# A hybrid decoder layer: weight transposes ahead of the scores, key and query splits on VectorE, attention operands loaded earlier

## The chip, the cores and the metric

The kernel runs on 1 core of one Trainium2 chip. The metric is the device time of one execution in microseconds. The kernel before took 1698.91 us (median of 3 runs, 1698.31 to 1705.39).

Engine names as in the profile: PE is TensorE's matmul, PEld its weight load, DVE VectorE, ACT ScalarE, POOL GpSimd, SP SyncE; SPq is SP's queue, from which most transfers are issued.

## The reference

One layer on 1024 tokens of width 1024, all in float32. The input projection feeds two mixers: a Mamba-2 scan of 16 heads (two groups, eight chunks of 128 tokens) and a causal differential attention of 8 heads. Both outputs, side by side 2048 wide, go through the output projection; a gated feed-forward block and norms follow.

```python
n = rmsnorm(h, mix_norm_w); proj = n @ w_in
y_ssd = ssd_mixer(proj[:, :SSD_PROJ], ...)          # chunked scan, gated norm
# attention, per head and block of 128 query rows: two score maps of depth 64
s = einsum("mbhqd,mbhkd->mbhqk", q, k)              # m = 0, 1; q scaled by 64**-0.5
p = softmax(where(causal, s, -inf)); w = p[0] - lam * p[1]
y_da = rmsnorm(w @ v, subln_w) * (1 - lambda_init)  # v is 128 wide
h = h + concat([y_ssd, y_da]) @ w_out
h = h + (silu(n2 @ w_gate) * (n2 @ w_up)) @ w_down  # n2 = rmsnorm(h)
return rmsnorm(h, final_norm_w)
```

## The kernel before

**Precision.** A float32 product is made of three matmuls of split operands. `split(hi, lo, raw)` casts `raw` to a shorter type on ACT (`hi`, the CAST of L173) and subtracts on another engine (`lo = raw - hi`, the TENSOR_TENSOR of L174). `mm3` (L119 to L121) then issues hi·hi, lo·hi and hi·lo. So every operand of a projection goes through a raw buffer, one ACT and one DVE instruction.

**Stages on the profile's axis.** To about 403 us: input norm, then the z, B, C, x and v projections, with the first group's scan woven in. 403 to 583 us: the k and q projections (8 calls of `pair_T`, 7 pieces each, 12 matmuls of 128x512 to a piece), with the second group's scan, `ssd_scan(1)`, woven in by `weave`: after the n-th piece, 30/50·n steps of the scan have been issued (L693 to L695). The scan writes its transposed output `y` to DRAM (`yT_d`), and k and q go to DRAM too. 583 to 969 us: attention. 969 to 1046 us: the rest of the output projection. From there the feed-forward block.

**Attention.** The loop at L940 runs over steps s; step s is head h = s // 8 and block i = s % 8 of 128 query rows; 64 such steps and 5 behind them drain. The step issues the two score maps of (h, i) (`att_front`: L769 with the queries' `QH`, L770 with their `QL`, L772 the causal mask), the row maximum on DVE (`nmx`, L774 or L776) and two exponentials on ACT (L778). Work of earlier rows follows, popped from a table `later` by a key: `att_mix` of row s-1 (DVE, L785 to L788: reciprocal `r`, factor `rr`, mixed weights into `p`), `att_turn` of row s-2 (PE transposes `wtp`, L798, copied back by ACT, L799), then filler matmuls, then `att_back` of row s-2 (PE, L804, output bank `o`), and `att_square`, `att_norm`, `att_out` of row s-3 or a group of four rows (`ms_o`, `of`, `oa` on DVE, transposes `otp`).

**Filler.** Between the turn and the back matmuls stand steps of the output projection (`filler`, `share`), each three matmuls of 128x256 into `po_s`. Phase 1 has 256 such steps, over the first two groups of `y` (y0 to y3, y4 to y7: `yh`, `yl`) with weights `wo0_*` and `wo1_*`; phase 2 has 128, over y8 to y11 (attention heads 0 to 3) with `wo2_*`. `share` gives phase 1 eight steps in each of s = 2 to 17 and 19 to 34, one call at s = 36 that only loads phase 2's operands, and four steps from s = 38 on.

**Orders.** PE's order in attention is that of the code (`manual_schedule` names PE only). The order of DVE, ACT, POOL and SP is fixed when the kernel is built, by a scheduler that plays the instructions through; the code's order is only its input.

**Buffers.** Tiles rotate in pools: P4 has 6 buffers of 4 KB per partition (probabilities `p` in attention), CV 4 (`kd`, `qd`, `v`), A4 14 (`KS`, `QH`, `QL`), B16 4 (`yh`, `yl`). A weight's raw tile, `wr_*`, has two buffers of its own (`load_raw`, L169), shared with the raws of y4 to y11.

**Keys and queries of a head** are loaded in two halves of 512 tokens (`qk_load`) and split (`qk_split`): KS is cast on ACT (L738), its other half-partitions become the low part by two 64x512 subtractions (L179), QH and QL come from `split`. For head 0 the subtractions run on DVE, for the others on GpSimd. Head h's half 0 is loaded at step 8(h-1) and split two steps later, half 1 is loaded at 3 and split at 5.

Of the kernel before, what the change touches and what calls it, by code (L numbers as in the profile page):

```python
# [9 lines left out]
F32 = mybir.dt.float32  # L10
# [7 lines left out]
P = 128  # L18
# [6 lines left out]
def tile_hybrid_block(  # L25
# [24 lines left out]
    nc = tc.nc  # L50
    DM = 1024
    T = 1024
    NT = T // P
# [100 lines left out]
    def CV(shape, dt, name):  # L154
        return cv.tile(shape, dt, tag="cv", name=name)
# [11 lines left out]
    def load_raw(src, shape, name):  # L167
        raw = wp.tile(shape, F32, tag="raw", bufs=2, name="wr_" + name)
        nc.sync.dma_start(raw, src)  # L169
        return raw  # L170
# [122 lines left out]
    nc.vector.memset(ones, 1.0)  # L293


    def w_unit(src, shape, name, alloc=None):
        raw = load_raw(src, shape, name)
        if alloc is None:
            hi = wp.tile(shape, F32R, tag="wh", bufs=3, name="wh_" + name)
            lo = wp.tile(shape, F32R, tag="wl", bufs=3, name="wl_" + name)  # L300
        else:
            hi, lo = alloc(shape, F32R, "wh_" + name), alloc(shape, F32R, "wl_" + name)
        split(hi, lo, raw)
        return hi, lo
# [376 lines left out]
    for col, name, sk in ((C_B, "B", sink_bc("B")), (C_C, "C", sink_bc("C")), (C_X, "x0", sink_x(0)),  # L681
# [3 lines left out]
        if name == "C":  # L685
# [6 lines left out]
    parity[0] = 1  # L692
    weave([(lambda c=c, d=d, n=n, h=h, sc=sc: pair_T(c + h * P, f"{n}{h}", sink_T(d, h), sc), 7)  # L693
           for h in range(0, NH, 2) for c, d, n, sc in ((C_K, kT_d, "k", None), (C_Q, qT_d, "q", 0.125))],
          ssd_scan(1), 30 / 50)  # L695


    cneg = hx.tile([P, P], F32, tag="hx", name="cneg")
# [20 lines left out]

    def qk_load(h, half):  # L720
        sl = slice(half * 512, half * 512 + 512)
        kd, qd = [CV([P, 2, 512], F32, f"{n}d{h}_{half}") for n in "kq"]
        for t_, src in ((kd, kT_d), (qd, qT_d)):
            sv = src[h].rearrange("(m d) t -> d m t", d=64)
            for r in (0, 64):
                nc.sync.dma_start(t_[r:r + 64, :, :], sv[:, :, sl])
        return kd, qd

    def qk_split(h, half, kd, qd):

        eng = nc.gpsimd if h else nc.vector
        ks = A4([P, 2, 512], F32R, f"KS{h}_{half}")
        qh = A4([P, 2, 512], F32R, f"QH{h}_{half}")
        if h or half:
            ql = A4([P, 2, 512], F32R, f"QL{h}_{half}")
        else:
            ql = wp.tile([P, 2, 512], F32R, tag="wl", bufs=3, name=f"QL{h}_{half}")
        nc.scalar.copy(ks, kd)  # L738
        for m in range(2):
            b = slice(64 - 64 * m, 128 - 64 * m)  # L740
            sub(ks[b, m, :], kd[b, m, :], ks[b, m, :].bitcast(F32), eng=eng)
        split(qh, ql, qd, eng)
        return ks, qh, ql
# [47 lines left out]
    def att_turn(h, i, pm):  # L791
        n = f"{h}_{i}"
        wT = pm[1]
        for j0 in range(0, i + 1, 4):
            j1 = min(i + 1, j0 + 4)
            pt = MS([P, 512], f"wtp{n}_{j0}")
            for j in range(j0, j1):
                nc.tensor.transpose(pt[:, (j - j0) * P:(j - j0 + 1) * P], pm[0][:, j * P:(j + 1) * P], ident)  # L798
            nc.scalar.copy(wT[:, j0 * P:j1 * P], pt[:, :(j1 - j0) * P])  # L799

    def att_back(h, i, pm, vt, o):
        wT = pm[1]
        for j in range(i + 1):
            nc.tensor.matmul(o[:, i % 4, :], wT[:, j * P:(j + 1) * P], vt[j], start=(j == 0), stop=(j == i))  # L804
# [13 lines left out]
    def att_out(h, q, oa):  # L818
        pt = MS([P, 512], f"otp{h}_{q}")
        for j in range(4):  # L820
            nc.tensor.transpose(pt[:, j * P:(j + 1) * P], oa[:, j, :], ident)
        if h >= NH // 2:
            if not y3:
                y3.extend(B16([P, 4, T], f"y{e}3") for e in "hl")
            hi, lo = [y[:, h - NH // 2, q * 512:q * 512 + 512] for y in y3]
            sl = pcol[:, SL:SL + 1]
            nc.scalar.mul(hi, pt, sl)
            nc.vector.scalar_tensor_tensor(lo, pt, sl, hi.bitcast(F32), op0=ALU.mult, op1=ALU.subtract)
            return
        oT = oa.rearrange("p j d -> p (j d)")  # L830
        nc.scalar.mul(oT, pt, pcol[:, SL:SL + 1])
        nc.sync.dma_start(yT_d[8 + h, :, q * 512:q * 512 + 512], oT)


    KG = 4
    NG = 16 // KG

    def load_y(kg):
        yh, yl = B16([P, KG, T], f"yh{kg}"), B16([P, KG, T], f"yl{kg}")
        for j in range(KG):  # L840
            kt = kg * KG + j
            if kg == 0:
                raw = P4([P, T], F32, f"wr_y{kt}")
                nc.sync.dma_start(raw, yT_d[kt])
            else:
                raw = load_raw(yT_d[kt], [P, T], f"y{kt}")
            split(yh[:, j, :], yl[:, j, :], raw)
        return yh, yl

    def wo_unit(kg, cg, alloc=None):  # L850
        src = w_out2[kg * KG * P:(kg + 1) * KG * P, cg * 256:cg * 256 + 256].rearrange("(k p) c -> p k c", p=P)
        return w_unit(src, [P, KG, 256], f"wo{kg}_{cg}", alloc)

    def out_steps(t, kys, ws, name, bank=MM):

# [16 lines left out]
    def filler():  # L872

        for kgs in ((0, 1), (2,)):
            nxt = [wo_unit(kg, 0) for kg in kgs]
            ys = [load_y(kg) for kg in kgs]
            yield
            for cg in range(4):
                cc = slice(cg * 256, cg * 256 + 256)
                ws = nxt  # L880
                for t in range(0, NT, 2):
                    if t == 6 and cg < 3:
                        nxt = [wo_unit(kg, cg + 1) for kg in kgs]
                    hx_t = hx.tile([P, 2, 256], F32, tag="hx", name=f"hx_{cg}_{t}_{kgs[0]}")
                    nc.sync.dma_start(hx_t, (h_d if kgs[0] else xh)[:, t:t + 2, cc])
                    steps = out_steps(t, ys, ws, f"s{kgs[0]}{cg}")
                    for q in range(2 * KG * len(kgs)):
                        ps = next(steps)
                        if q == 2 * KG * len(kgs) - 1:
                            nc.vector.tensor_tensor(hx_t, ps, hx_t, op=ALU.add)  # L890
                            nc.sync.dma_start(h_d[:, t:t + 2, cc], hx_t)
                        yield
# [4 lines left out]
    later = {}  # L897

    def at(step, f):
        later.setdefault(step, []).append(f)  # L900
# [16 lines left out]
    split_of(0, 1)  # L917
    for h in range(1, NH):
        s0 = (h - 1) * NT
        for d, f, a in ((0, raw_of, (h, 0)), (2, split_of, (h, 0)), (3, raw_of, (h, 1)), (4, v_of, (h,)),  # L920
                        (5, split_of, (h, 1))):
            at(s0 + d, lambda f=f, a=a: f(*a))
    ROWS = NH * NT

    def fill_up(n):
        for _ in range(n):
            next(fill, None)

    def share(s):

        if 2 <= s < 18 or 19 <= s < 35:
            fill_up(8)
        elif s == 36:
            fill_up(1)
        elif 38 <= s < ROWS:
            fill_up(4)
        elif s >= ROWS:
            fill_up(8)

    with tc.manual_schedule(engines={mybir.EngineType.PE}):  # L940
        for s in range(ROWS + 5):
            h, i = divmod(s, NT)
            if h < NH:
                pm, sm = att_front(h, i, [heads[h][0], heads[h][1]])
                if i % 4 == 0:
                    o = psum["oo"].tile([P, 4, P], F32, tag="oo", name=f"o{h}_{i // 4}")
                    oa = ob.tile([P, 4, P], F32, tag="ob", name=f"oa{h}_{i // 4}")
                    sso = small.tile([P, 4], F32, tag="sso", bufs=2, name=f"sso{h}_{i // 4}")
                    r4 = small.tile([P, 4, 2], F32, tag="r4", bufs=2, name=f"r4{h}_{i // 4}")
                vt = heads[h]["v"]  # L950
                at(s + 1, lambda h=h, i=i, pm=pm, sm=sm, r4=r4: att_mix(h, i, pm, sm, r4[:, i % 4, :]))
                at(s + 2, lambda h=h, i=i, pm=pm: att_turn(h, i, pm))
                at(s + 2.5, lambda h=h, i=i, pm=pm, vt=vt, o=o: att_back(h, i, pm, vt, o))
                at(s + 3, lambda h=h, i=i, pm=pm, o=o, r4=r4, sso=sso: att_square(h, i, pm, o, r4, sso))
                if i % 4 == 3:
                    at(s + 3, lambda h=h, q=i // 4, o=o, oa=oa, r4=r4, sso=sso: att_norm(h, q, o, oa, r4, sso))
                    at(s + 4.5, lambda h=h, q=i // 4, oa=oa: att_out(h, q, oa))
            for f in later.pop(s, []):
                f()
            share(s)  # L960
            for f in later.pop(s + 0.5, []):
                f()
        ws = [wo_unit(3, 0)]
        for _ in fill:
            pass
# [19 lines left out]
    ys = [y3]  # L985
# [329 lines left out]
```

## Time and profile before

| | |
|---|---|
| runs | 1698.31, 1698.91, 1705.39 us |
| profiled execution | 1696.42 us, span 1694.7 us, mean granted clock 0.975 |
| PE | busy 1588.5 us, 94% of the span |
| DVE, ACT, POOL | 1129.5 (67%), 802.4 (47%), 568.2 us (34%) |
| k/q projections, 403.00 to 583.20 | 180.20 us, PE busy 179.86 |
| attention, 583.20 to 969.00 | 385.8 us |
| rest of the output projection, 969.00 to 1046.00 | 77.00 us, PE busy 76.03 |

A stage's window has its length, then the busy time of each engine with its count of instructions, then the clock granted to TensorE as a share of full speed. What PE can gain in a stage is its idle time (length less busy) and the time that it ran at a lower clock.

### The profile page before, as it was taken

How to read it: one execution, taken by the hardware profiler on the slowest of the kernel's cores; microseconds unless marked ns; L12 is line 12 of the kernel's file. 1: busy time of each engine (PE TensorE's matmuls, PEld its weight loads, DVE VectorE, ACT ScalarE, POOL GpSimd, SP SyncE). 2: the span in 40 equal slices, each digit the busy share in tenths (PEclk: the TensorE clock that was granted, in tenths of full speed). 3: DMA queues.
4: the chain of work that ended last, by engine and by line, in shares of the span. 5: the costliest groups of instructions: out<-in, count | busy, mean ns of one | idle time of the engine just before them, and what ended most of it. 6: DMA issues, size and time to landing. Idle time of an engine off the chain costs nothing. (4 is left out here: it accounts for less than half of the span.)

```text
span 1694.7 us, 24141 instructions
## 1 busy us (share of the span) xinstructions
PE 1588.5 (94%) x9034; PEld 1379.4 (81%) x9034; DVE 1129.5 (67%) x1597; ACT 802.4 (47%) x1659; POOL 568.2 (34%) x412
## 2 busy tenths in 40 slices
PE   5999989999999879899789998999999999999997
PEld 4977889898878769899678898888888888778886
DVE  8666787776665565556766658655555555698987
ACT  4544666544444455555665524433333333334445
POOL 5113233234333042222221024444444445542422
PEclk9999999999999979999899999999999999999999
DMA  4213345645545585434433242322332232963222
GB/s 164 88 49 115 109 129 170 190 137 170 169 145 176 157 224 151 122 103 131 156 106 119 91 139 91 105 94 93 107 106 94 93 106 97 358 247 119 99 100 99
DMA packets 160798, 225.24 MB, mean 133 GB/s; under 512 B 10581, under 2 KB 121242, under 8 KB 159274
## 3 DMA queue, kind: packets, MB, share of 16 engines
q1 hardware_dynamic: 157050, 210.53, 38.3%
q0 software_dynamic: 3632, 13.17, 2.5%
q8 instruction: 71, 1.16, 0.3%
q14 instruction: 45, 0.37, 0.1%
HBM read 156.23 MB, written 67.44 MB: 132 GB/s over the span
## 5 line engine op out<-in xcount | busy, mean ns | idle before, releaser
L120 PE MATMUL x<-n,wa 128*128 128x512 f32 x352 | 137.4, 390 | 0.0
L119 PE MATMUL x<-n,wa 128*128 128x512 f32 x352 | 137.3, 392 | 0.0
L121 PE MATMUL x<-n,wa 128*128 128x512 f32 x352 | 136.2, 390 | 0.0
L119 PE MATMUL po_s<-wh_wo,yh 128*128 128x256 f32 x384 | 116.4, 303 | 7.7 <-ACT yh L173 7.7
L173 ACT CAST wa<-s 128x512 fp32r<-128x512 f32 x88 | 54.8, 622 | 130.2 <-PE x L121 58.5
L121 PE MATMUL po_s<-wh_wo,yl 128*128 128x256 f32 x384 | 110.9, 289 | 4.1 <-DVE yl L174 4.1
L778 ACT ACTIVATE p<-s,nmx 128x256 f32<-128x256 f32 (+7 forms) x128 | 94.7, 743 | 42.4 <-DVE nmx L774 26.4
L120 PE MATMUL po_s<-wl_wo,yh 128*128 128x256 f32 x384 | 110.6, 288 | 1.7 <-DVE wl_wo L174 1.7
L174 DVE TENSOR_TENSOR wa<-s,wa 128x512 fp32r<-128x512 f32 x88 | 76.9, 875 | 47.3 <-ACT wa L173 47.0
L804 PE MATMUL o<-v,p 128*128 128x128 f32 x576 | 79.8, 284 | 25.6 <-ACT p L778 7.9
L173 ACT CAST dg<-gd 128x512 fp32r<-128x512 f32 x77 | 47.8, 622 | 113.2 <-PE dx L121 55.6
L804 PEld LDWEIGHTS o<-v,p 128*128 128x128 f32 x576 | 71.7, 195 | 29.6 <-issue 10.5
L769 PE MATMUL s<-KS,QH 128*128 128x512 f32 (+2 forms) x192 | 79.3, 413 | 5.3 <-ACT QH L173 3.2
L119 PEld LDWEIGHTS po_s<-wh_wo,yh 128*128 128x128 f32 x384 | 75.4, 196 | 8.8 <-ACT yh L173 8.8
L121 PEld LDWEIGHTS po_s<-wh_wo,yl 128*128 128x128 f32 x384 | 75.2, 196 | 5.2 <-DVE yl L174 5.2
L174 DVE TENSOR_TENSOR dg<-gd,dg 128x512 fp32r<-128x512 f32 x77 | 63.4, 827 | 23.5 <-ACT dg L173 23.5
L121 PEld LDWEIGHTS x<-n,wa 128*128 128x128 f32 x352 | 66.4, 189 | 13.9
L119 PEld LDWEIGHTS x<-n,wa 128*128 128x128 f32 x352 | 66.4, 189 | 13.6
L120 PEld LDWEIGHTS x<-n,wa 128*128 128x128 f32 x352 | 66.4, 189 | 13.6
L120 PEld LDWEIGHTS po_s<-wl_wo,yh 128*128 128x128 f32 x384 | 75.6, 197 | 1.9 <-DVE wl_wo L174 1.9
L774 DVE TENSOR_REDUCE nmx<-s 128x1 f32<-128x640 f32 (+3 forms) x64 | 63.8, 1019 | 12.7 <-PE s L772 12.1
L120 PE MATMUL dx<-dw,dg 128*128 128x512 f32 x176 | 67.9, 392 | 2.8 <-DVE dw L174 2.7
(491 smaller groups left out, 5213.7 us busy)
## 6 DMA issues: line engine op xcount, KB each, us to landing
gd<-g_d SPq DMA_DIRECT2D x11, 1792.0 KB, 10.1
wr_g<-in_w_gate_dram SPq DMA_DIRECT2D x22, 512.0 KB, 3.6
wr_u<-in_w_up_dram SPq DMA_DIRECT2D x22, 512.0 KB, 3.7
g_d<-sg SPq DMA_DIRECT2D x22, 512.0 KB, 2.6
wr_d<-in_w_down_dram SPq DMA_DIRECT2D x22, 512.0 KB, 6.7
L<-cs_d POOLq DMA_DIRECT2D x16, 512.0 KB, 4.5
kd<-kT_d SPq DMA_DIRECT2D x32, 256.0 KB, 4.3
wr_wo<-in_w_out_dram SPq DMA_DIRECT2D x16, 512.0 KB, 3.9
```

The costliest lines, as they stand in the source:

```text
L119: nc.tensor.matmul(ps, lh, rh, start=first, stop=False, skip_group_check=more)
L120: nc.tensor.matmul(ps, lh, rl, start=False, stop=False, skip_group_check=more)
L121: nc.tensor.matmul(ps, ll, rh, start=False, stop=last, skip_group_check=more)
L173: nc.scalar.copy(hi, raw)
L174: eng.tensor_tensor(lo, raw, hi.bitcast(F32), op=ALU.subtract)
L769: nc.tensor.matmul(sc, qh[:, m, qr], ks[:, m, :w], start=True, stop=False)
L774: nc.vector.reduce_max(nmx[:, m:m + 1], s[:, :Lk], axis=AX.X, negate=True)
L778: nc.scalar.activation(pm[m][:, :Lk], ss[m][:, :Lk], AF.Exp, bias=nmx[:, m:m + 1], accum_out=sm[:, m:m + 1])
L804: nc.tensor.matmul(o[:, i % 4, :], wT[:, j * P:(j + 1) * P], vt[j], start=(j == 0), stop=(j == i))
```

## The change

Eight edits, most of them in attention and what leads up to it.

1. The raws of `wo0_0`, `wo1_0` and of y4 to y7 go to P4 buffers (y0 to y3 were there already), so they need not take turns in the two raw buffers. The filler loads its first group of `y`, then the weights, then the other group; in phase 2 it loads y8 to y11 ahead of `wo2_0`.
2. The scan's second weave is 30/42 where it was 30/50: the scan is used up after 42 pieces.
3. Head 0's first half of keys and queries is loaded into P4 where it was CV.
4. `qk_split` is on DVE for all heads (28 KS subtractions and 14 QL subtractions move from POOL).
5. The next head's halves are loaded two steps earlier (half 0) and one step earlier (half 1), and half 0 is split one step earlier.
6. `share`: eight filler steps in s = 2 to 37 except each head's last row (s % 8 = 7), phase 2's load at s = 38 (was 36), four steps from s = 40; seven (was eight) in the drain.
7. `att_turn` of row s-2 is issued ahead of the scores of step s, where it stood behind them.
8. The keys of `att_back` and `att_out` change from .5 to .25, which leaves their place in a step.

```diff
-    def w_unit(src, shape, name, alloc=None):
-        raw = load_raw(src, shape, name)
+    def w_unit(src, shape, name, alloc=None, raw=None):
+        if raw is None:
+            raw = load_raw(src, shape, name)
+        else:
+            raw = raw(shape, F32, "wr_" + name)
+            nc.sync.dma_start(raw, src)
...
-          ssd_scan(1), 30 / 50)
+          ssd_scan(1), 30 / 42)
...
-        kd, qd = [CV([P, 2, 512], F32, f"{n}d{h}_{half}") for n in "kq"]
+        kd, qd = [(CV if h or half else P4)([P, 2, 512], F32, f"{n}d{h}_{half}") for n in "kq"]
...
-        eng = nc.gpsimd if h else nc.vector
+        eng = nc.vector
...
-            if kg == 0:
+            if kg < 2:
                 raw = P4([P, T], F32, f"wr_y{kt}")
...
-            nxt = [wo_unit(kg, 0) for kg in kgs]
-            ys = [load_y(kg) for kg in kgs]
+            ys = [load_y(kgs[0])]
+            nxt = [wo_unit(kg, 0, None, P4 if kg < 2 else None) for kg in kgs]
+            ys += [load_y(kg) for kg in kgs[1:]]
...
-        for d, f, a in ((0, raw_of, (h, 0)), (2, split_of, (h, 0)), (3, raw_of, (h, 1)), (4, v_of, (h,)),
+        for d, f, a in ((-2, raw_of, (h, 0)), (1, split_of, (h, 0)), (2, raw_of, (h, 1)), (4, v_of, (h,)),
                         (5, split_of, (h, 1))):
-            at(s0 + d, lambda f=f, a=a: f(*a))
+            at(max(0, s0 + d), lambda f=f, a=a: f(*a))
...
-        if 2 <= s < 18 or 19 <= s < 35:
+        if 2 <= s < 38 and s % NT != 7:
             fill_up(8)
-        elif s == 36:
+        elif s == 38:
             fill_up(1)
-        elif 38 <= s < ROWS:
+        elif 39 < s < ROWS:
             fill_up(4)
         elif s >= ROWS:
-            fill_up(8)
+            fill_up(7)
...
             h, i = divmod(s, NT)
+            for f in later.pop(s - 0.5, []):
+                f()
             if h < NH:
...
-                at(s + 2, lambda h=h, i=i, pm=pm: att_turn(h, i, pm))
-                at(s + 2.5, lambda h=h, i=i, pm=pm, vt=vt, o=o: att_back(h, i, pm, vt, o))
+                at(s + 1.5, lambda h=h, i=i, pm=pm: att_turn(h, i, pm))
+                at(s + 2.25, lambda h=h, i=i, pm=pm, vt=vt, o=o: att_back(h, i, pm, vt, o))
```

The four places of the program where the instructions' order changes most. In the rows, a name's last number tells one use of a buffer from another.

ACT's rows around the last pieces of the k/q projections (`wa_q`, `o_q` belong to them). Before: the second group's `y` (`yh_5281`) is not there yet; `KS`, `QH` of head 0 and the first output weights (`wh_wo`) stand between the last pieces, and the first of `yh_5281` comes behind two rows of exponentials (L778).

```order
L173 CAST wa_q_3_5169<-wr_q_1_5075 128x512
L329 ACTIVATE o_q_1_5079<-z_q_5134 128x512
L173 CAST wa_q_4_5186<-wr_q_1_5075 128x512
L711 ACTIVATE lexp<-lexp 128x2
L738 CAST KS_0_5243<-kd_0_5237 128x1024
L173 CAST wh_wo_0_5253<-wr_wo_0_5251 128x1024
L329 ACTIVATE o_q_1_5079<-x_q_5082 128x512
L173 CAST QH_0_5244<-qd_0_5238 128x1024
L173 CAST wh_wo_0_5259<-wr_wo_0_5257 128x1024
L778 ACTIVATE p_0_5320,sm_0_5318<-s_0_5319,nmx_0_5317 128x128 x2
L738 CAST KS_1_5307<-kd_1_5301 128x1024
```

After, the same stretch:

```order
L173 CAST wa_q_3_5169<-wr_q_1_5075 128x512
L173 CAST yh_5281<-wr_y_5283 128x1024
L333 ACTIVATE o_q_1_5079<-z_q_5134 128x512
L173 CAST wa_q_4_5186<-wr_q_1_5075 128x512
L173 CAST yh_5281<-wr_y_5287 128x1024
L173 CAST yh_5281<-wr_y_5291 128x1024
L173 CAST wh_wo_0_5271<-wr_wo_0_5269 128x1024
L173 CAST yh_5281<-wr_y_5295 128x1024
L173 CAST wh_wo_0_5277<-wr_wo_0_5275 128x1024
L715 ACTIVATE lexp<-lexp 128x2
L333 ACTIVATE o_q_1_5079<-x_q_5082 128x512
L173 CAST wh_wo_1_5837<-wr_wo_1_5835 128x1024
```

The four casts of y4 to y7 and those of both first weights have moved ahead of the last piece's end.

PE at attention's step 2, before: the scores of row 2 (`s_2`), then the turn of row 0 (`wtp`), then filler.

```order
L769 MATMUL s_2_5359<-KS_0_5243,QH_0_5244 128x384
L770 MATMUL s_2_5359<-KS_0_5243,QL_0_5245 128x384
L772 MATMUL s_2_5359<-mask 128x128
L798 MATMUL wtp_0_0_5378<-ident,p_0_5320 128x128
L119 MATMUL po_s_0_5387<-wh_wo_0_5253,yh_5263 128x256
```

After:

```order
L776 MATMUL s_1_5342<-mask 128x128
L802 MATMUL wtp_0_0_5365<-ident,p_0_5320 128x128
L773 MATMUL s_2_5370<-KS_0_5243,QH_0_5244 128x384
L774 MATMUL s_2_5370<-KS_0_5243,QL_0_5245 128x384
L776 MATMUL s_2_5370<-mask 128x128
```

The turn now stands between two rows' scores, and filler follows the scores.

DVE in head 0 between the mixed weights of rows 4 and 5, before:

```order
L788 SCALAR_TENSOR_TENSOR p_4_0_5472<-p_4_1_5480,rr_4_5571,p_4_0_5472 128x640
L774 TENSOR_REDUCE nmx_5_5535<-s_5_0_5537 128x1
L774 TENSOR_REDUCE nmx_5_5535<-s_5_1_5545 128x1
L785 RECIPROCAL r_1_5492<-sm_5_5536 128x2
L787 TENSOR_SCALAR rr_5_5642<-r_1_5492,neglam,sm_5_5536 128x1
```

After:

```order
L792 SCALAR_TENSOR_TENSOR p_4_0_5477<-p_4_1_5485,rr_4_5571,p_4_0_5477 128x640
L179 TENSOR_TENSOR KS_0_5822<-kd_0_5633,KS_0_5822 64x512 x2
L778 TENSOR_REDUCE nmx_5_5541<-s_5_0_5543 128x1
L778 TENSOR_REDUCE nmx_5_5541<-s_5_1_5551 128x1
L174 TENSOR_TENSOR QL_0_5824<-qd_0_5634,QH_0_5823 128x1024
```

The next head's two KS subtractions stand ahead of row 5's maxima, and its QL behind them.

DVE where phase 2's operands are loaded, before (`yl` is y9 to y11; the low part of `wo2_0` stands 46 rows further up, in head 3):

```order
L174 TENSOR_TENSOR yl_7679<-wr_y_7684,yh_7678 128x1024
L774 TENSOR_REDUCE nmx_4_7636<-s_4_0_7638 128x1
L785 RECIPROCAL r_0_7415<-sm_3_7600 128x2
L787 TENSOR_SCALAR rr_3_7669<-r_0_7415,neglam,sm_3_7600 128x1
L788 SCALAR_TENSOR_TENSOR p_3_7602<-p_3_7602,rr_3_7669 128x512
L774 TENSOR_REDUCE nmx_4_7636<-s_4_1_7646 128x1
L174 TENSOR_TENSOR yl_7679<-wr_y_7688,yh_7678 128x1024
```

After, at step 39 (row 7 of head 4):

```order
L174 TENSOR_TENSOR yl_7766<-wr_y_7775,yh_7765 128x1024
L789 RECIPROCAL r_1_7611<-sm_6_7728 128x2
L791 TENSOR_SCALAR rr_6_7826<-r_1_7611,neglam,sm_6_7728 128x1
L792 SCALAR_TENSOR_TENSOR p_6_0_7730<-p_6_1_7738,rr_6_7826,p_6_0_7730 128x896
L174 TENSOR_TENSOR yl_7766<-wr_y_7779,yh_7765 128x1024
L174 TENSOR_TENSOR wl_wo_0_7786<-wr_wo_0_7783,wh_wo_0_7785 128x1024
L778 TENSOR_REDUCE nmx_7_7804<-s_7_0_7806 128x1
L778 TENSOR_REDUCE nmx_7_7804<-s_7_1_7814 128x1
```

The low part of `wo2_0` has come down behind y11's, ahead of row 7's maxima.

More of the change, by code (lines that the diff above doesn't have):

```diff
@@ L848, in load_y, with wo_unit @@
         return yh, yl
-    def wo_unit(kg, cg, alloc=None):
+    def wo_unit(kg, cg, alloc=None, raw=None):
         src = w_out2[kg * KG * P:(kg + 1) * KG * P, cg * 256:cg * 256 + 256].rearrange("(k p) c -> p k c", p=P)
-        return w_unit(src, [P, KG, 256], f"wo{kg}_{cg}", alloc)
+        return w_unit(src, [P, KG, 256], f"wo{kg}_{cg}", alloc, raw)
     def out_steps(t, kys, ws, name, bank=MM):
@@ L956, in tile_hybrid_block @@
                     at(s + 3, lambda h=h, q=i // 4, o=o, oa=oa, r4=r4, sso=sso: att_norm(h, q, o, oa, r4, sso))
-                    at(s + 4.5, lambda h=h, q=i // 4, oa=oa: att_out(h, q, oa))
+                    at(s + 4.25, lambda h=h, q=i // 4, oa=oa: att_out(h, q, oa))
             for f in later.pop(s, []):
@@ L960, in tile_hybrid_block @@
             share(s)
-            for f in later.pop(s + 0.5, []):
+            for f in later.pop(s + 0.25, []):
                 f()
```

## The prediction

> **What bounds the kernel now.** I read the page first, then the stages, then PE's waits stage by stage, then the timeline at each wait.
>
> ```profile
> span 1694.7 us, 24141 instructions
> PE 1588.5 (94%) x9034; PEld 1379.4 (81%) x9034; DVE 1129.5 (67%) x1597; ACT 802.4 (47%) x1659; POOL 568.2 (34%) x412
> ```
>
> PE is the bound; time can come only from its 106 idle us and from stretches at a lower clock. The stages, in order: start of the first 30/42 weave, k/q projections, attention's steps 0 to 4, steps 5 to 34, 35 to 41, 42 to 63, the rest of the output projection; last, a stretch behind one gap.
>
> ```profile
> core 0: us, PE busy (x) PEld busy (x) DVE busy (x) ACT busy (x) POOL busy (x), PEclk, DMA share, GB/s
> 225.70:403.00 177.30, 166.46 (x1244) 156.15 (x1244) 130.95 (x153) 99.02 (x219) 60.57 (x44) 0.97 0.52 162
> 403.00:583.20 180.20, 179.86 (x843) 144.98 (x841) 115.11 (x165) 86.75 (x196) 58.10 (x50) 1.00 0.49 154
> 583.20:625.40 42.20, 24.87 (x124) 21.57 (x124) 24.80 (x32) 23.51 (x43) 14.65 (x9) 0.68 0.95 252
> 625.40:808.20 182.80, 175.04 (x1382) 169.34 (x1381) 106.95 (x179) 102.95 (x256) 47.14 (x31) 0.99 0.44 128
> 808.20:849.10 40.90, 29.63 (x179) 26.24 (x179) 27.96 (x41) 25.78 (x56) 11.69 (x6) 0.87 0.46 149
> 849.10:969.00 119.90, 107.50 (x797) 101.50 (x795) 83.41 (x147) 71.56 (x188) 18.45 (x17) 0.96 0.31 100
> 969.00:1046.00 77.00, 76.03 (x604) 73.81 (x605) 47.49 (x88) 27.01 (x72) 20.88 (x22) 1.00 0.40 131
> 859.40:866.10 6.70, 6.70 (x31) 6.31 (x31) 3.12 (x7) 3.41 (x9) 4.20 (x3) 0.54 0.05 14
> ```
>
> PE's idle time is 0.3 us in the k/q projections, 17.3 in steps 0 to 4, 7.8, 11.3 and 12.4 in the three stretches of attention behind them, 1.0 at the end. The granted clock adds at most (1 - clock) x length: 13.5, 1.8, 5.3, 4.8 us in the four stretches of attention. So all of attention holds some 74 us; everything else that the change touches is full.
>
> **Start, steps 0 to 4.** PE's waits in 583.2 to 625.4, largest first, with their sum, count and longest, then the rows around them:
>
> ```profile
> PE po_s L119 <- ACT yh L173: 7.7, 4, 3.7
> PE po_s L121 <- DVE yl L174: 4.1, 4, 1.6
> PE s L769 <- ACT QH L173: 3.2, 1, 3.2
> PE s L769 <- ACT p L778: 1.5, 2, 0.8
> ...
> 567.43 3.89 ACT L173 CAST yh<-wr_y 128x1024 fp32r<-128x1024 f32 x4
> 569.76 4.62 DVE L174 TENSOR_TENSOR yl<-wr_y,yh 128x1024 fp32r<-128x1024 f32 x4
> 582.87 0.39 PE L121 MATMUL x_q<-nn,wa_q 128*128 128x512 f32 x1
> 589.00 0.59 SPq L169 DMA_DIRECT2D wr_y<-yT_d  x1
> 608.98 1.04 ACT L173 CAST yh<-wr_y 128x1024 fp32r<-128x1024 f32 x1 [0.69 <-DMA wr_y<-yT_d]
> 625.46 0.48 PE L769 MATMUL s<-KS,QH 128*128 128x512 f32 x1
> ```
>
> The first filler block needs y0 to y7. y0 to y3 are split by 574.4, but y4 is asked for only at 589.00, since the two raw buffers hold the first weights, and the third of the four is cast at 608.98. The 124 matmuls of this stretch would take 124 x 175.04/1382 = 15.7 us at the next stretch's pace, so 42.2 - 15.7 = 26.5 us are lost here.
>
> After, y4 to y7 have P4 buffers that y0 to y3 free at about 574, their transfers stand on SP's queue ahead of head 0's `v` and the last stores of q, and their casts stand on ACT ahead of the projections' end. DVE pays 1.2 us each there (4.62/4), in a stretch where it is busy 64%. So the two largest waits go, and QH's too, as its raw is loaded earlier into P4. What stays, as estimates:
> - The first turn now follows the scores of row 1 at once and waits for row 0's maximum, exponential and mixing. The rows bound it by 0 and by the three small waits' kind (3.2 + 1.5); I take 4.3, near the upper end, as nothing is left to cover it.
> - The next head's keys are cast on ACT early, in an order that puts a cast waiting for its transfer ahead of row 3's exponentials. One transfer's landing bounds it; I take 4.4, by this row of the page:
>
> ```profile
> kd<-kT_d SPq DMA_DIRECT2D x32, 256.0 KB, 4.3
> ```
>
> - Some 1 us at the lower clock behind these gaps.
>
> 26.5 - 9.7 = 16.8, rounded up to 18, because the first scores start behind no QH wait and the last scan work has left DVE. Term: **-18** (from -26, nothing stays, to -9, where yh's and yl's 11.8 us and 5 us of low clock stay).
>
> **Denser scan weave.** The scan's work is the same, used up 14 pieces sooner; PE is full there, so the gain is nothing in itself and the risk is a wait. The first group's weave has the same 30/42, and of its 10.8 idle us these two are the scan's:
>
> ```profile
> PE ytp L627 <- DVE S L605: 2.0, 1, 2.0
> PE yp L608 <- DVE y L597: 1.7, 1, 1.7
> ```
>
> Term: **+1** (0 to +3.7); these pieces are longer matmuls than the first weave's and cover more.
>
> **Steps 5 to 34.** PE's waits in 625.5 to 808, and DVE around one of them:
>
> ```profile
> PE o L804 <- issue: 4.4, 1, 4.4
> PE po_s L120 <- DVE wl_wo L174: 1.7, 1, 1.7
> ...
> 761.15 3.42 DVE L174 TENSOR_TENSOR wl_wo<-wr_wo,wh_wo 128x1024 fp32r<-128x1024 f32 x1
> 765.62 1.21 DVE L174 TENSOR_TENSOR wl_wo<-wr_wo,wh_wo 128x1024 fp32r<-128x1024 f32 x1
> ```
>
> The 4.4 us stand at step 18, which has no filler, between a turn and its back matmuls; the change gives it eight steps. The same subtraction took 3.42 us beside a GpSimd QL and 1.21 alone: with the splits off GpSimd, the 1.7 us go. Back come steps 7, 15, 23 and 31, now without filler, where back matmuls wait for the turn's copy with only scores in between: about half a microsecond each (estimate). -6.1 + 2.1 = **-4** (-7 to 0).
>
> DVE's new work:
>
> ```profile
> L179 POOL TENSOR_TENSOR KS<-kd,KS x28: 1260/1272/2189, 602.4 to 865.5; 64x512 fp32r<-64x512 f32 x28
> L179 DVE TENSOR_TENSOR KS<-kd,KS x2: 683/686/689, 593.6 to 594.3; 64x512 fp32r<-64x512 f32 x2
> L174 POOL TENSOR_TENSOR QL<-qd,QH x14: 2347/2400/3377, 605.0 to 884.5; 128x1024 fp32r<-128x1024 f32 x14
> L174 DVE TENSOR_TENSOR QL<-qd,QH x2: 1218/1222/1226, 586.5 to 598.7; 128x1024 fp32r<-128x1024 f32 x2
> ```
>
> 28 x 0.686 + 14 x 1.222 = 36.3 us, 2.6 per half of a head, over seven heads. In steps 5 to 34 DVE goes from 59% to about 70% of the stretch: hidden behind PE, unless a row's maximum stands behind a split (a rival below). The Trainium skill ("SBUF — State Buffer", section "Who interferes with whom") says that a VectorE instruction with two SBUF inputs and a GpSimd instruction that reads SBUF exclude each other; the trace agrees (3.42 against 1.21 us). By that rule DVE would get back on average more than one such excess, and the net price of the move would be nearer to 25 than 36 us; the sum would not change, as the work is hidden.
>
> **Steps 35 to 41, the change of phases.** PE's waits in 808.2 to 849, then rows:
>
> ```profile
> PE o L804 <- ACT p L799: 7.6, 4, 3.4
> PE o L804 <- DVE oa L814: 2.5, 1, 2.5
> ...
> 817.69 0.53 SPq L169 DMA_DIRECT2D wr_y<-yT_d  x1
> 822.48 1.04 ACT L173 CAST yh<-wr_y 128x1024 fp32r<-128x1024 f32 x1 [4.01 <-DMA wr_y<-yT_d]
> 824.94 0.58 PE L804 MATMUL o<-v,p 128*128 128x128 f32 x1 [3.39 <-ACT p L799]
> ```
>
> Three steps without filler pass one by one, while ACT stands in front of a `y` that is not there. 11.3 + 5.3 = 16.6 us are lost. After, only 38 and 39 lack filler, but y10 and y11 and then `wo2_0` pass through the two raw buffers in turn: issue to cast is 822.48 - 817.69 = 4.8, cast 1.0, subtraction 1.2, so 7 us each turn, and DVE has `wl_wo2_0` ahead of row 39's maxima. I expect two turns less the scores between them, about 15: **-1** (-8, if only one turn shows, to +6, if two and the old output-bank wait of 2.5 do and the clock stays low).
>
> **Steps 42 to 63.** PE's waits in 849.1 to 969.5:
>
> ```profile
> PE o L804 <- ACT p L778: 6.4, 3, 2.6
> PE o L804 <- DVE r L785: 2.1, 1, 2.1
> ```
>
> The 6.4 us fall on row 6 of heads 5 to 7, where the squares' sum (`ms_o`) of a group stands late on DVE; it comes earlier now. Four filler steps cover less than eight, and DVE, 70% busy, gets 5.2 us per head more. I take half of the 6.4 less 1: **-2** (-8 to +8: the two rows gone, or 2.6 us at two or three halves uncovered).
>
> The low clock counts here: 859.40 to 866.10, behind a 2.6 us gap, ran at 0.54. The Trainium skill ("TensorE: Matmul & The Clock Gate", section "What's actually happening") puts the half clock behind an idle window of about 3.4 us; here shorter gaps did it, and the measurement decides. By the rule no low clock hangs on these gaps, and the gain here would be 1 us smaller.
>
> The rest of the output projection takes seven instead of eight steps per drain step; PE is full there: 0.
>
> **Sum:** -18 + 1 - 4 - 1 - 2 = -24, about -23 with the four 0.5 us estimates rounded up. Against the profiled execution 1696.42 - 23 = 1673.4; that execution lies 2.5 below the median of the runs, so **1676**.
>
> **Rivals.**
> - *More is hidden.* The start loses only 3 (-23), the phase change 7 us less than before, steps 42 on 5 less: -38, about 1661. For it: the filler really covers 35 to 37. Against it: DVE's and ACT's orders put conversions ahead of exponentials at both places.
> - *The start gains half.* In steps 0 to 4 the transfers are busy 95% at 252 GB/s, and y4 to y7 with two weights are 3 MB, 12 us at that rate. If they land 10 us later than I think, PE waits at step 2 as before: -8 there, -13 in all, about 1686. Against it: their place on SP's queue is ahead of that crowd.
> - *Slower: splits in front of maxima.* In head 0 DVE has the next head's two KS rows ahead of row 5's maxima. If each half's 2.6 us reaches PE, 14 x 2.6 = 36 us against 24: about 1711. It decides from 24/14 = 1.7 us per half. Against it: filler of eight steps (24 matmuls, some 3 us) and DVE 30 to 41% idle.
> - *Nothing moves.* The same filler runs out elsewhere, and waits only change places: about 1698. Against it: the start's 11.8 us hang on two buffers that are no longer shared.
>
> **Chances.** Forecast 0.52 (its own range 1667 to 1688); more hidden 0.15; half the start 0.15; slower 0.09; nothing 0.09. Half a per cent, 8.5 us, is about what runs of this kernel can tell from no change. Faster by more: 0.52 + 0.15 + 0.11 = 0.78; within: 0.04 + 0.09 = 0.13; slower 0.09. The range leaves out the slower case, most of "nothing" and the lowest few in a hundred: 1660 to 1694.
>
> **What would show it.** Right: row 5 of head 0 starts some 17 us earlier, no wait of `po_s` for `yh` or `yl` in the first steps, no 4 us gap at step 18, splits of 0.69 and 1.22 us on DVE. Still there: waits of 3 to 5 us around steps 38 to 40. Wrong: `yh` of y4 to y7 cast after 595; `nmx` rows waiting behind KS or QL with PE idle at the same time; new waits of `ytp` or `yp` ahead of attention.

## The result and the profile after

The changed kernel took 1678.41 us (median of 4 runs, 1677.68 to 1680.29); the kernel before, run beside it, 1700.47. The ratio is 0.9868, with a 95% interval of 0.9843 to 0.9893: 1.3% faster. 1676 was forecast, with 1660 to 1694 around it. The profiled execution of the changed kernel took 1680.29 us, 16.1 less than that of the kernel before; the traces below account for those 16.1 us, the runs for some 22.

The page of the changed kernel, first its head:

```profile
span 1678.6 us, 24065 instructions
PE 1578.7 (94%) x9034; PEld 1373.6 (82%) x9034; DVE 1154.2 (69%) x1639; ACT 802.1 (48%) x1659; POOL 493.8 (29%) x370
```

DVE has 24.7 us more to do and GpSimd 74 us less. The work that moved costs DVE 36 us by the price of its rows. The difference fits DVE's own subtractions, which no longer stretch beside GpSimd: one of y or of an output weight took up to 3.42 us before, at most 1.23 after.

The stages, each from and to the same instruction in both kernels: k/q projections from their second piece (`y_k`) on, steps 0 to 4, 5 to 34, 35 to 40, 41 to 62, and from row 63 to the filler's last matmul (the drain).

```profile
core 0: us, PE busy (x) PEld busy (x) DVE busy (x) ACT busy (x) POOL busy (x), PEclk, DMA share, GB/s
403.17:589.40 186.23, 183.00 (x849) 147.34 (x847) 130.10 (x171) 92.67 (x203) 59.08 (x51) 0.99 0.54 175
589.40:614.40 25.00, 18.61 (x130) 17.86 (x129) 19.27 (x34) 15.23 (x36) 0.00 (x0) 0.86 0.79 225
614.40:790.80 176.40, 166.92 (x1309) 160.94 (x1308) 118.32 (x202) 103.84 (x256) 8.09 (x8) 0.99 0.43 130
790.80:833.40 42.60, 33.18 (x233) 31.69 (x232) 33.39 (x49) 27.63 (x60) 1.01 (x1) 0.88 0.50 157
833.40:939.90 106.50, 96.78 (x747) 91.89 (x745) 77.74 (x139) 64.89 (x174) 9.66 (x10) 1.00 0.34 105
939.90:966.80 26.90, 23.16 (x185) 21.94 (x183) 12.69 (x18) 10.50 (x22) 3.81 (x5) 1.00 0.50 159
```

Of the kernel before, the first stage and the last two. (The prediction's first window begins at 403.00, which is not the same instruction in the two kernels; the stages between stand there.)

```profile
401.54:583.20 181.66, 181.32 (x849) 146.21 (x847) 116.57 (x165) 87.34 (x197) 59.48 (x51) 1.00 0.49 155
849.10:960.80 111.70, 100.74 (x749) 95.49 (x747) 77.36 (x139) 65.59 (x175) 17.94 (x16) 0.95 0.33 104
960.80:982.10 21.30, 19.86 (x163) 19.11 (x162) 10.20 (x15) 9.28 (x21) 3.07 (x4) 1.00 0.47 150
```

Filler moved between the stages, 24 matmuls at a time. A row 7 with them lasted 7.32 us before (from 686.09 to 693.41), one without 4.89 us after (678.63 to 683.52), so 24 are worth about 2.4 us, by an estimate (2.6 against the same row with edit 6 undone, 7.50 us). The account:

| stage | before | after | difference | less filler moved | forecast |
|---|---|---|---|---|---|
| ahead of the k/q projections' second piece | 401.5 | 403.2 | +1.6 | +1.6 | 0 |
| k/q projections from there | 181.7 | 186.2 | +4.6 | +4.6 | +1 |
| steps 0 to 4 | 42.2 | 25.0 | -17.2 | -17.2 | -18 |
| steps 5 to 34 | 182.8 | 176.4 | -6.4 | +0.8 (3 x 24 fewer) | -4 |
| steps 35 to 40 | 40.9 | 42.6 | +1.7 | -3.1 (2 x 24 more) | -1 |
| steps 41 to 62 | 111.7 | 106.5 | -5.2 | -5.2 | -2 |
| row 63 to last filler | 21.3 | 26.9 | +5.6 | +3.2 (24 more) | 0 |
| behind it, to the end | 712.6 | 711.8 | -0.8 | -0.8 | 0 |

The stretch from 849.1 on, in the prediction "steps 42 to 63", begins with row 41. The differences add up to -16.1. The start came as forecast; 5 us were lost ahead of it, 5 in steps 5 to 34 and 3 in the drain that were not forecast, and 5 more won in between. The 1.6 us of the first line are no effect of the change that could be named: nothing is edited there, and the traces of three variants that differ only in attention reach that instruction at 400.9, 404.7 and 407.5 us.

PE's waits, stage by stage in the same order (sum, count, longest; the last line stands 1 us behind the last stage):

```profile
PE x_q L119 <- DVE o_q L340: 3.1, 1, 3.1
...
PE s L773 <- ACT p L782: 4.1, 1, 4.1
PE wtp L802 <- DVE p L792: 1.6, 1, 1.6
...
PE o L808 <- ACT p L782: 5.7, 4, 2.3
PE o L808 <- DVE oa L818: 2.9, 1, 2.9
...
PE wtp L802 <- DVE yl L832: 5.7, 1, 5.7
PE o L808 <- DVE oa L818: 3.7, 1, 3.7
...
PE wtp L802 <- ACT p L803: 2.9, 2, 1.5
...
PE po_s L119 <- DVE hx L895: 2.3, 3, 0.8
...
PE po_b L119 <- DVE hx L895: 0.8, 1, 0.8
```

The 11.8 us of `po_s` waiting for `yh` and `yl` are gone, as are the 4.4 us at step 18 and the filler's 1.7 us for `wl_wo`. The first row is new, and the prediction has nothing like it. Rows of DVE, PE and ACT around it:

```profile
579.60 1.23 DVE L174 TENSOR_TENSOR yl<-wr_y,yh 128x1024 fp32r<-128x1024 f32 x1
583.80 0.29 DVE L712 TENSOR_TENSOR lv<-lv 128x128 f32<-128x128 f32 x1 [2.97 <-DMA lv<-in_lam_k_dram]
584.01 0.68 DVE L340 SCALAR_TENSOR_TENSOR o_q<-x_q,o_q 128x512 f32<-128x512 f32 x1
...
584.84 0.75 PE L119 MATMUL x_q<-nn,wa_q 128*128 128x512 f32 x1 [3.08 <-DVE o_q L340]
...
584.90 1.05 ACT L173 CAST yh<-wr_y 128x1024 fp32r<-128x1024 f32 x1 [3.30 <-DMA wr_y<-yT_d]
```

DVE stood idle for 2.97 us in front of the product of the lambda vectors (`lv`), whose transfer now follows y4 to y6 on SP's queue. The sum that empties a bank for the projections' last piece was queued behind it, and PE waited.

### The profile page after: what moved, and what is told of

Same layout as the page of the kernel before. It is cut to its first block, busy times and chain, and to the rows that moved or that the text cites. A ratio compares the mean times of both kernels' runs of the same rounds, so it can differ in the third digit from the quotient of the medians.

```text
span 1678.6 us, 24065 instructions
## 1 busy us (share of the span) xinstructions
PE 1578.7 (94%) x9034; PEld 1373.6 (82%) x9034; DVE 1154.2 (69%) x1639; ACT 802.1 (48%) x1659; POOL 493.8 (29%) x370
## 5 line engine op out<-in xcount | busy, mean ns | idle before, releaser
L96 POOL TENSOR_TENSOR rs_o<-ms_o,mhalf 128x4 f32<-128x4 f32 x16 | 16.8, 1053 | 333.0 <-DVE ms_o L94 333.0
L773 PE MATMUL s<-KS,QH 128*128 128x512 f32 (+2 forms) x192 | 75.1, 391 | 6.3 <-ACT p L782 5.3
L778 DVE TENSOR_REDUCE nmx<-s 128x1 f32<-128x640 f32 (+3 forms) x64 | 63.6, 1017 | 17.9 <-PE s L776 17.6
```

The lines of the kernel that those rows point to most:

```text
L96: nc.gpsimd.tensor_tensor(r, ms, mhalf[:, :w], op=ALU.pow)
L773: nc.tensor.matmul(sc, qh[:, m, qr], ks[:, m, :w], start=True, stop=False)
L778: nc.vector.reduce_max(nmx[:, m:m + 1], s[:, :Lk], axis=AX.X, negate=True)
```

## Experiments

Each is an edit of the changed kernel, timed against the kernel before in the same rounds. The changed kernel itself has the ratio 0.9868; 0.001 is 1.7 us. Edits 2, 3 and 8 were not undone one by one.

**Edit 1 undone** (y4 to y7 and first weights back in the two raw buffers).

```diff
-            if kg < 2:
+            if kg == 0:
...
-            ys = [load_y(kgs[0])]
-            nxt = [wo_unit(kg, 0, None, P4 if kg < 2 else None) for kg in kgs]
-            ys += [load_y(kg) for kg in kgs[1:]]
+            nxt = [wo_unit(kg, 0) for kg in kgs]
+            ys = [load_y(kg) for kg in kgs]
```

> The changed kernel with edit 1 undone: y4 to y7 and the first weights share the two raw buffers again, weights ahead of y. Theory (the start's gain hangs on those two buffers): +14 to +20 us against the changed kernel's 1678.4, waits of po_s for yh and yl of some 10 us in head 0 return, row 5 starts at 625 or later instead of 614. Rival (the gain comes from the earlier key loads and the denser scan): at most +5.

1688.68 us, ratio 0.9927 (0.9911 to 0.9943): +10, between the two. Its waits from the projections' end to row 5:

```profile
PE po_s L119 <- ACT yh L173: 4.7, 2, 3.0
PE wtp L802 <- DVE p L792: 4.5, 1, 4.5
PE po_s L121 <- DVE yl L174: 1.2, 2, 0.7
```

The waits for y are back, but only 5.9 us of the old 11.8: row 5 starts at 617.2, not at 625. From row 0 to row 5 this run takes 32.7 us and the changed kernel 24.3, so edit 1 wins 8.4 us there, about half of the start's gain. The prediction hung all of the 11.8 us on the two buffers; half of them stay away through the other edits. The k/q stretch of the table lasts 181.5 us here, as in the kernel before, against 186.2: the lambda wait is gone. So edit 1 itself brings the new loss ahead of the start, and the denser scan, which this run keeps, costs nothing there. Behind row 5 the run is 6 us longer than the changed kernel, at a lower clock (0.96 against 0.99 in steps 5 to 34), so its +10 is not what the start alone wins.

**Edit 7 undone** (turn behind the scores).

```diff
-                at(s + 1.5, lambda h=h, i=i, pm=pm: att_turn(h, i, pm))
+                at(s + 2, lambda h=h, i=i, pm=pm: att_turn(h, i, pm))
```

> The changed kernel with the turn back behind the scores (edit 7 undone). Theory: the filler hides the copy in filled steps, so it shows only in the steps without filler (7, 15, 23, 31, 38, 39), where the back matmuls wait for ACT's copies, 1 to 1.5 us each: +4 to +8 us. Rival (the early turn costs waits for the mixing and the transposes' bank, as the 5.7 us at step 39 and 1.4 us at rows 7 of heads 5 and 6): -2 to -5.

1694.39 us, 0.9956 (0.9941 to 0.9971): +16, more than either expected. Its waits from 600 to 800 us:

```profile
PE o L808 <- ACT p L803: 7.4, 5, 2.1
PE o L808 <- DVE r L789: 6.5, 1, 6.5
PE otp L825 <- ACT p L803: 6.2, 4, 1.5
```

The sign and the place (rows 7) are the theory's, the size isn't: each unfilled row 7 costs twice, 1.5 us in its own step and about 1.9 us two steps later. Neither wait is in the changed kernel, whose rows 7 run without a gap; it waits at rows 2 instead, which are free of waits here. The 6.5 us stand at row 6 of head 0, which the theory doesn't name and where the changed kernel waits 2.9. And only part of the 16 us is attention's: from row 0's scores to the filler's last matmul the trace takes 388.1 us, that of the changed kernel 376.7, so 11.4 more. Another 4.3 us stand ahead of the k/q projections' second piece (407.5 against 403.2), where this edit changes nothing.

**Edit 6 undone** (old filler distribution).

```diff
-        if 2 <= s < 38 and s % NT != 7:
+        if 2 <= s < 18 or 19 <= s < 35:
             fill_up(8)
-        elif s == 38:
+        elif s == 36:
             fill_up(1)
-        elif 39 < s < ROWS:
+        elif 38 <= s < ROWS:
             fill_up(4)
         elif s >= ROWS:
-            fill_up(7)
+            fill_up(8)
```

> The changed kernel with the old distribution of filler (edit 6 undone: filler in rows 7, none at 18 and 35 to 37, phase 2 from 38, eight steps in the drain). Theory: with the early turn rows without filler cost little, but the change of phases again has three unfilled rows in a row while y waits, and step 18 its bank wait: +3 to +9 us; the drain gives back 3. Rival (all the filler has to be run anyway and gaps only move): within 2 us.

1688.96 us, 0.9931 (0.9909 to 0.9953): +10.6, by the theory's mechanism and a little above its range. Step 18 waits 4.7 us for the output bank again, step 36 5.6 us, step 38 4.8 us.

**Edits 6 and 7 both undone.**

```diff
-        if 2 <= s < 38 and s % NT != 7:
+        if 2 <= s < 18 or 19 <= s < 35:
...
-                at(s + 1.5, lambda h=h, i=i, pm=pm: att_turn(h, i, pm))
+                at(s + 2, lambda h=h, i=i, pm=pm: att_turn(h, i, pm))
```

> The changed kernel with edits 6 and 7 both undone: old filler distribution and the turn behind the scores. Alone, the first undoing cost 10.6 us (1689.0) and the second 16.0 us (1694.4). Theory (the two belong together: the early turn pays only where a row has no filler, which the new distribution makes of rows 7): much less than the sum, 1687 to 1692. Rival (each is worth its amount by itself): the sum, about 1705, slower than before.

1691.69 us, 0.9943 (0.9921 to 0.9964). The sum of the two is excluded: they belong together. The traces show it better than the times: from row 0's scores to the filler's last matmul the changed kernel takes 376.7 us, and 387.6 with edit 6 undone, 388.1 with edit 7 undone, 387.6 with both undone. There, neither edit wins anything without the other. Filler taken from rows 7 fills steps 18 and 35 to 37, and the early turn makes rows 7 cheap without it. Together they are worth 0.9943 - 0.9868, some 13 us; the other six edits the other 10.

**Edit 4 undone** (splits of heads 1 to 7 on GpSimd).

```diff
-        eng = nc.vector
+        eng = nc.gpsimd if h else nc.vector
```

> The changed kernel with the key and query splits of heads 1 to 7 back on GpSimd (edit 4 undone). Theory: DVE's 36 us are hidden behind PE, and GpSimd's subtractions only stretch DVE's beside them: +1 to +4 us, with DVE rows of L174 up to 3.4 us. Rival (splits ahead of maxima and of the group norm on DVE cost PE time: the 2.9 us at step 6, the 2 us at rows 2): -4 to -8, and these waits go.

1681.78 us, 0.9883 (0.9866 to 0.9901): +3, as the theory has it, though the intervals overlap. The rival is out in its sign: the waits at rows 2 did not go (2.0 to 2.6 us each), and DVE's 36 us were indeed hidden in the main. Only the 2.9 us at step 6 fell, to 1.5, and the wait at step 39 to 2.5.

**Edit 5 undone** (old load steps).

```diff
-        for d, f, a in ((-2, raw_of, (h, 0)), (1, split_of, (h, 0)), (2, raw_of, (h, 1)), (4, v_of, (h,)),
+        for d, f, a in ((0, raw_of, (h, 0)), (2, split_of, (h, 0)), (3, raw_of, (h, 1)), (4, v_of, (h,)),
```

> The changed kernel with the next head's key and query loads at their old steps (edit 5 undone). Theory: the early loads make the scheduler put key casts, which then wait for their transfers, ahead of row 3's exponentials and row 3's square on ACT: the waits at steps 4 (4.1 us) and 6 (2.9 us) and the low clock behind each go, -4 to -9 us. Rival (ACT's order there comes from something else, the transfers' crowd after the projections): within 2 us of 1678.4, waits of the same size.

1681.98 us, 0.9883 (0.9857 to 0.9909): no gain, so the theory fell. Step 4's wait became 2.3 us, step 6's 3.5 in two parts. The wait at step 4 is real (ACT, changed kernel):

```profile
604.31 1.04 ACT L742 CAST KS<-kd 128x1024 fp32r<-128x1024 f32 x1 [1.75 <-DMA kd<-kT_d]
...
605.98 0.70 ACT L782 ACTIVATE p<-s,nmx 128x512 f32<-128x512 f32 x1
...
607.49 0.79 PE L773 MATMUL s<-KS,QH 128*128 128x512 f32 x1 [4.15 <-ACT p L782]
```

A key cast stands in front of row 3's exponentials and waits for its transfer, and PE waits 4.15 us. But the load's place in the code does not set that order: with the old steps the scheduler puts the same cast in front of the same exponentials, and it waits 1.52 us.

**The lambda wait**, three ways. First the vectors loaded and reduced ahead of the projections: the block from `lv = CV(...)` to `neglam` stands ahead of the second `weave`.

```diff
+    lv = CV([P, 4, 64], F32, "lv")
...
+    nc.vector.tensor_scalar(neglam, lexp[:, 1:2], LAMBDA_INIT, lexp[:, 0:1], op0=ALU.subtract, op1=ALU.subtract)
     weave.done = 0
     parity[0] = 1
...
```

> The changed kernel with the lambda vectors loaded and reduced ahead of the k/q projections instead of behind them; nothing else is edited. Theory: PE's 3.1 us wait in the last piece of the projections is DVE standing at the lambda product for its transfer, with q's sum (L340) queued behind; it goes with the low clock behind it: -4 to -5 us, to about 1674, row 0's scores at about 585 instead of 590. Rival (the y splits on DVE ahead of that sum make the wait, or the y transfers do): within 1 us, and the wait stays at 2 to 3 us.

1686.45 us, 0.9912 (0.9894 to 0.993): slower. The 3.1 us wait went, as the theory says, but the vectors' transfers, now ahead of the scan's `bc` on SP's queue, made PE wait 2.8 us for `bc` at 411, and row 0 waited 4.0 us for ACT. Second, the arithmetic on GpSimd, the transfer in its place:

```diff
-    nc.vector.tensor_tensor(lv[:, 0:2, :], lv[:, 0:2, :], lv[:, 2:4, :], op=ALU.mult)
+    nc.gpsimd.tensor_tensor(lv[:, 0:2, :], lv[:, 0:2, :], lv[:, 2:4, :], op=ALU.mult)
+    for w in (32, 16, 8, 4, 2):
+        nc.gpsimd.tensor_tensor(lv[:, 0:2, :w], lv[:, 0:2, :w], lv[:, 0:2, w:2 * w], op=ALU.add)
...
```

> The changed kernel with the lambda vectors' product, sums (as halving additions) and difference on GpSimd where they were on DVE; the transfer stays where it is. DVE's other rows keep their order. Theory: PE's 3.1 us wait in the last piece of the projections is DVE standing in front of that product; with DVE free of it q's sum runs at once, the wait and the low clock behind it go: -3 to -5 us against 1678.4, row 0's scores at 585 to 587. Rival (y5 to y7's conversions, queued on DVE ahead of the same sum, wait for their transfers as long): within 1 us.

1679.88 us, 0.9874 (0.9849 to 0.99): the same time. PE's waits from 580 to 592 us:

```profile
PE s L775 <- ACT o_q L333: 3.7, 1, 3.7
PE x_q L119 <- DVE o_q L340: 0.9, 1, 0.9
```

and ACT's rows there:

```profile
585.10 1.05 ACT L173 CAST yh<-wr_y 128x1024 fp32r<-128x1024 f32 x1 [1.57 <-DMA wr_y<-yT_d]
588.36 0.20 ACT L717 ACTIVATE lexp<-lexp 128x2 f32<-128x2 f32 x1 [2.20 <-POOL lexp L716]
...
589.40 0.59 ACT L333 ACTIVATE o_q<-x_q 128x512 f32<-128x512 f32 x1
```

The wait fell from 3.1 to 0.9 us: most of it was DVE in front of the lambda product. And a wait of 3.7 us came at row 0, since ACT had y7's cast, the lambdas' exponential and a weight's cast ahead of the copy that empties the projections' last bank. Third, the vectors in a spare buffer, loaded ahead of the second `weave`; their product then runs at 350.7 us.

```diff
-    lv = CV([P, 4, 64], F32, "lv")
+    lv = hx.tile([P, 4, 64], F32, tag="hx", name="lv")
...
```

> The changed kernel with the lambda vectors loaded into another buffer ahead of the k/q projections, so that their product stands some 200 rows earlier on DVE and their exponential as early on ACT; no stall for them is left near attention on either engine. Theory: with DVE and ACT both free of the lambda wait, row 0 starts 3 to 5 us earlier than in the changed kernel (590): 585 to 587, -3 to -4 us. Rival (ACT's casts of y7 and of the next keys, which wait for their transfers, stand ahead of the copy that empties the projections' last bank, and hold row 0): the wait moves to row 0 as in the variant with GpSimd, within 1 us.

1680.79 us, 0.9869 (0.984 to 0.9898): as the rival has it. With no lambda left near attention, ACT's y7 cast and a key cast ahead of that copy waited for their transfers, and row 0 waited 4.1 us. So the new wait's first cause is the lambda transfer, and behind it stands another of the same size, set by y7's landing and ACT's order. In these variants that bounds what edit 1 can win.

**Phase 2's weights ahead of y8 to y11** (order as before the change).

```diff
-            ys = [load_y(kgs[0])]
+            ys = [] if kgs[0] else [load_y(kgs[0])]
             nxt = [wo_unit(kg, 0, None, P4 if kg < 2 else None) for kg in kgs]
+            if kgs[0]:
+                ys = [load_y(kgs[0])]
```

> The changed kernel with phase 2's weights asked for ahead of y8 to y11 (as before the change), all else kept. Theory: the 12.9 us lost at steps 38 to 41 (waits of 3.7 and 5.7 us and the low clock behind them) are two turns of two raw buffers, y10 and y11 and then wo2_0; with wo2_0 split long before, the second turn goes: -3 to -5 us, the wait at step 39 under 2 us. Rival (y10 and y11's landing alone sets it): within 1 us.

1683.0 us, 0.9888 (0.9863 to 0.9913): the theory fell; step 39 waits 6.0 us. In the trace ACT now casts the next two weights there, waiting 1.6 and 1.4 us for transfers, ahead of the copy that frees the transposes' bank. The raw buffers that `wo2_0` leaves are taken by the next in line. The order on ACT matters more: in the traces with edit 1 or edit 4 undone the second of these casts stands behind row 39's first exponential, and the wait at step 39 is 2.3 and 2.5 us.

**Early turn only below row 40.**

```diff
-                at(s + 1.5, lambda h=h, i=i, pm=pm: att_turn(h, i, pm))
+                at(s + (1.5 if s < 40 else 2), lambda h=h, i=i, pm=pm: att_turn(h, i, pm))
```

> The changed kernel with the early turn for rows of s below 40 only; from there the turn is behind the scores as before. Theory: with four filler steps and no unfilled rows the early turn only exposes waits for the transposes' bank and the group norm (1.4 and 0.9 us at rows 7 and 6 of heads 5 to 7): -3 to -4 us against 1678.4. Rival (those waits come from the chain's length and move behind the scores): within 1 us.

1677.99 us, 0.9867 (0.9842 to 0.9893). In its trace steps 42 to 62 are 4.9 us shorter, as the theory has it, but row 63 to the end is 3.0 us longer: row 61's turn now falls behind the last scores, and a transpose in the drain waits 2.2 us where the changed kernel's waits 1.4. The sum is not told from the changed kernel.

**The same, with eight filler steps in the drain.**

```diff
-            fill_up(7)
+            fill_up(8)
```

> The changed kernel with the early turn only for rows of s below 40 (as in the variant that ran at 1678.0) and eight filler steps in the drain where the change has seven. Theory: behind the last head the one bank of the filler is full at the end of each block of eight, and with seven steps to a drain step the next block starts at once and waits 0.78 us for the sum on DVE, four times; with eight, transposes and back matmuls stand between two blocks and the four waits go: -3 us against the early-turn variant, -3 to -6 against the changed kernel, 1673 to 1676. Rival (PE has no other work left in the drain, so the sum's 0.78 us is waited for elsewhere): within 1 us of 1678.

1677.69 us, 0.9855 (0.9839 to 0.9872), the lowest ratio of all, but not clear of 0.9868, and above the 1673 to 1676 expected. The drain's waits:

```profile
PE po_s L119 <- DVE hx L895: 0.9, 1, 0.9
PE po_b L119 <- DVE hx L895: 0.3, 1, 0.3
```

Against 3.1 us in four: that part is as expected, and row 63 to the end is 3.1 us shorter than in the early-turn variant. From row 0's scores to the filler's last matmul its trace takes 372.4 us, 4.3 less than the changed kernel's; the runs don't tell the two apart.

## Why the prediction came out right, and where its steps did not

1676 was forecast and 1678.41 measured, but that closeness is partly luck. Between the two profiled executions, the pair that the terms speak of, the gain is 16.1 us, not the sum's 24: 14 us came out worse than the terms and 6 better. The runs gain 22 because the profiled execution of the kernel before lies 4 us below its median in these rounds, that of the changed kernel 2 us above its own.

- **Start: right, half of it for its reason.** -17.2 us against -18. Row 3's exponentials behind a key cast cost 4.1 us, forecast 4.4. Two misses cancel: the first turn's wait was 1.6, not 4.3, and the low clock took more than the 1 us assumed (0.86 over 25 us is at most 3.5). The claim that the two raw buffers carry the 11.8 us of y waits was too strong: with them back, half of these stay away, and no run isolates which other edit does that. Row 5 starts 11 us earlier than before, not 17, for what was lost ahead of it.
- **The stretch ahead of the start: the failed step.** The forecast's only term there was the denser scan, +1 (0 to +3.7), with the scan's own waits as its price. That price came out at nothing: no wait of `ytp` or `yp` showed, and with edit 1 undone the stretch is as long as before. The stretch still grew by 4.6 us, and the miss lies in edit 1's working: "DVE pays 1.2 us each there" counted the work of the moved rows, but not what the moved transfers pushed back on SP's queue (the lambda vectors), nor what stood behind the waiting instruction on DVE. The GpSimd variant shows it, 3.1 to 0.9 us. The wait of 3.1 us and the low clock behind it (0.83 from 580 to 590, at most 1.7 us; the matmul there took 0.75 us, 0.39 before) cover the 4.6.
- **Steps 5 to 34: wrong sign**, +0.8 against -4. The 4.4 and 1.7 us went as forecast. What came back was looked for at rows 7, where there is no wait; it stands at rows 2 (5.7 us in four) and at row 6 of head 0 (2.9 us), where the output bank waits for the group norm. Rows 2 of heads 3 and 4 wait because rows 7 lack filler: with the old distribution steps 26 and 34 have no wait and last 4.2 us each, here 6.4 and 5.1. For heads 1 and 2 that run doesn't show it: step 10 still waits, and step 18 has no filler there.
- **Change of phases: right within its bounds**, -3.1 against -1. The 5.7 us at step 39 are not `wo2_0`'s turn in the raw buffers, as the prediction had it: with that turn gone 6.0 were left. They are ACT's casts, waiting for whatever transfer comes next, ahead of the copy that frees a bank.
- **Steps 41 to 62: too small, and for another reason**, -5.2 against -2. PE's idle time fell only from 11.0 to 9.7 us; the other 4.0 are the same matmuls at a clock of 1.00 where it was 0.95. The prediction put its 6.4 us on rows 6 of heads 5 to 7, but 2.6 of them are at row 2 of head 5 and stayed at 2.4. Rows 6 waited 1.9 to 2.1 us each and now wait 0.6 to 0.9, as forecast; new waits of 1.5 and 1.4 us at rows 7 of heads 5 and 6 took part of that back.
- **Drain: missed**, +3.2 against 0: waits of 0.78 us for one bank, three in the stage and one behind it, since seven steps no longer match a block of eight. The last variant shows it.
- **The rivals.** "Slower" is excluded by undoing edit 4, "half the start" and "nothing" by the stages. "More is hidden" did not come: the start and the change of phases, where it had its gain, kept waits of 4 to 6 us.

## What to carry to other kernels

When transfers are moved ahead on a queue, list those that they pass and find on each engine the instruction that waits for one of these: what is queued behind it pays. Move filler and the order of dependent steps together, since the one decides what the other is worth: undone alone they cost 10.6 and 16 us, undone together 13, and within attention, in the traces, each of the three costs some 11. A wait taken off one engine often had another of its size behind it; three ways of removing a 3 us wait won nothing.

## What the runs showed of the hardware

A broadcast of four vectors of 64 numbers is not a short transfer: it took 5.9 to 7.2 us from issue to landing among 512 KB transfers (3.5 to 5.0 before the change). The last of its four issues ended at 576.92, and DVE started on it at 583.80.

The clock did not answer to a gap's length alone: behind 2.6 us it ran at 0.54 for 6.7 us in the kernel before, while the changed kernel ran at 1.00 throughout steps 41 to 62 with a gap of 2.4 us in them. Over all traces here, from 600 to 1000 us, the clock was below 0.80 in the 6.5 us behind each of PE's 37 waits of more than 3.0 us. Of the 48 waits between 2.0 and 3.0 us, 17 left it at 1.00: it fell to 0.74 behind 2.01 us (edit 4 undone, step 34) and stayed at 1.00 behind 2.98 us (phase 2's weights first, step 6). The Trainium skill ("TensorE: Matmul & The Clock Gate", section "What's actually happening") puts the half clock behind an idle window of about 3.4 us, with free-running windows; the 2.6 us gap does not agree with that length, and no run here tells where such a window began.
